# P1's results on a second queue, B21 cast earlier, kept blocks in u's place, four operands not kept (soft mixture of experts)

## The chip, the cores and the metric

One core of a Trainium2 chip runs the whole kernel; seven more cores are idle. The metric is the device time of one execution in microseconds, of which several are taken. Before: a median of 1366.94 us over 3 runs (1365.35 to 1368.19).

The engines have names in the profile: PE (TensorE, matmuls; PEld its weight loads), DVE (VectorE), ACT (ScalarE), POOL (GpSimd), SP (SyncE, which only issues transfers). Transfers are issued from three queues, those of SP, ACT and POOL. Each engine and each queue works in the order of the program.

## The reference

```python
probs = softmax(router_logits)              # 16 x 512 tokens, 8 experts
output = zeros((16, 512, 2048))
for e in range(8):
    output += probs[:, :, e:e+1] * (x @ expert_weights[e])     # 512 -> 2048
```

Since the experts' results are added, this is one matrix product: an operand of 8192 tokens by 8 x 512 columns (x times the token's probability for each expert) with the 4096 x 2048 stacked weights. x, the probabilities and the weights are float32; the kernel multiplies in float16 and adds in float32.

## The kernel before

**Seven products in place of eight.** The product is cut in two in each direction (tokens: even and odd blocks of 256; experts: 0 to 3 and 4 to 7; columns: two halves of 1024), and Winograd's form of Strassen's scheme makes seven products of these quarters, here called P1 to P7 (`r` in the code). `product(r, q)` makes product r for token pair q (0 to 15). Each of these is cut once more into seven: its `steps` 1, 5, 6, 2, 7, 3, 4, each of eight matmuls with 512 columns, write the results (0,0), (0,1), (1,0), (1,1) of 128 tokens by 512 columns. Where two products of a stage allow it, steps 1 and 5 are cut a third time (`Third`): matmuls of 256 columns, with sums `s` of the left operands and `t` of the weights, and between them evacuations of one half of a bank onto the other (`ps<-ps,d` in the profile, parts x6, q6, x7, q7). Part x7 writes into the bank that the evacuation of x6 reads, so it waits for it.

**Stages.** A stage is one or two products, whose steps alternate; each step is a slot, so `(3,4)` is slot 4 of stage 3. `add` numbers the stages: P1 in stages 0 to 7, P2 from 6 to 14, P5 and P6 from 15 (`k5`) to 31 (`k7`), P7 and P4 from 31 to 47 (`k3`), P3 from 47 to 55. Stages 0 to 5, 8 to 13 and 49 to 54 have the third cut; in them the two last slots of the stage before are run between the parts (`held`). P1's operands come from x and the probabilities; P1 for q = 0 and 1 has been made before stage 0.

**Order.** The order on TensorE is written out. Transfers are hung on slots with `at(stage, slot, ...)`. VectorE's work that isn't an evacuation goes through a queue of tasks (`later`) with a planned cost; `slack` runs tasks from it as long as a planned clock of VectorE is behind that of TensorE, so a stage's operands are made during the stage before. Loads of x and probabilities (`start_loads`) are issued two stages ahead.

**What the change touches.**

- `sink` in `product`, r == 1: P1's four results of each product go to DRAM (`kept`), from POOL's queue, as soon as they are evacuated: (0,0) at step 2 and (1,0) at step 4 by ScalarE (`L627`), (1,1) and (0,1) at steps 7 and 3 by VectorE. P2 and P6 read them again.
- `Base.fetch`: reads such a block from SP's queue into an `h` tile (`half()`, 13 places, which hold results on their way out too). P2 and P6 add to it.
- tag `u`, one place of 4 KB in each partition: in P1 a room for loads of x (stages 3 to 5), in P7 and P3 the second product of an operand that is a difference. In P2 and P6 it is free.
- `cast21`, `CASTS`: the weights B21 are cast from float32 to float16 on their way in, from POOL's queue, in eight halves; P2's sums read them in stage 5. `wedge` loads two more halves of weights into one tile of 15 places (`w`), makes t1 and t2 of them on VectorE, and stores these; `WEDGES` says when: the first cast at its first pair of numbers, the second cast so many slots later as its last number says, the two tasks t1 and t2 at the pair between.
- `cast_odd`: casts of single halves, among them B21's block (0,1) again in stage 14.
- `KEEP` and `Left.store`: P6's left operand is a difference that P3 needs too. For q in `KEEP` both its halves (512 KB each) are stored in P6 from SP's queue and fetched again in P3 (`Operand`, 1 MB, from ScalarE's queue into a `w` tile), and P3 makes each half of its operand with two operations (`first`, `less`: product, difference). For other q, `left_of` takes the last line: four blocks are loaded (`xpool`, nine places), and each half takes three operations (`first`, `second` into `u`, `less`).

Of the kernel before, what the change touches and what calls it, by code (L numbers as in the profile page):

```python
# [31 lines left out]
def kernel(  # L32
# [7 lines left out]
    nc = tc.nc  # L40
    P = 128
    f16 = mybir.dt.float16
    f32 = mybir.dt.float32
# [33 lines left out]
    def half():  # L77
        return h_tile([P, NB], f32)
# [21 lines left out]
    def note(i):  # L100
        last[i.ins.engine] = i.ins
        if ordered[0]:
            tc.keep_in_program_order(i)
# [20 lines left out]

    def pool(o, i, **how):
        note(nc.gpsimd.dma_start(out=o, in_=i, **how))  # L126

    def bank():
        return psum.tile([P, NB], f32, name="ps", tag="ps")
# [433 lines left out]
    class Operand:  # L563
# [5 lines left out]
        def fetch(self):  # L569
            self.t = wpool.tile([P, 2, K8, HQ], f16, name="o", tag="w")  # L570
            note(nc.scalar.dma_start(out=self.t, in_=self.source))
# [160 lines left out]
    class Base:  # L732
# [2 lines left out]
        def __init__(self, source):  # L735
            self.source, self.t = source, {}

        def fetch(self, tn):
            self.t[tn] = half()
            sp(self.t[tn], self.source(tn))  # L740

        def __call__(self, tn):
# [16 lines left out]
    right = {r: Right() for r in (2, 5, 6, 7, 4, 3)}  # L759
    right[1] = Right(w, {p: Task(2.2, sums[p]) for p in (6, 7, 4)})  # L760
    lefts, xs, ps_, bases = {}, {}, {}, {}
    KEEP = range(1, 14)

    def xblock(h):
        if h not in xs:
# [34 lines left out]
    def product(r, q, **how):  # L800
        left, loads = left_of(r, q)
        lefts[r, q] = left
        p = None
        if r == 1:
            def sink(tn, o):
                pool(kept_rows(q)(tn), o)
            p = Product(right[1], left, sink)
        elif r == 2:
            if q >= 13:
                base = products[1, q].o.__getitem__  # L810
            else:
                base = bases[2, q] = Base(kept_rows(q))
            p = Product(right[2], left, to_out(q, 0, 0), base)
        elif r == 5:
            bases[6, q] = m1 = Base(kept_rows(q))
            m1.task = {}

            p = Product(right[5], left, to_out(q, 1, 0))
        elif r == 6:
            m1 = bases[6, q]  # L820

            def base(tn):
                need(m1.task[tn])
                return m1.t[tn]
            p = Product(right[6], left, to_out(q, 0, 1), base)
            if q in KEEP:
                left.kept = dram.tile([P, 2, K8, HQ], f16, name=f"kept_left_{q}")
        elif r == 7:
            if q < 14:
                base = bases[7, q] = Base(lambda tn: out_rows(q, 0, 1, tn))  # L830
            else:
                base = products[6, q].o.__getitem__
            p = Product(right[7], left, to_out(q, 1, 1), base)
        elif r == 4:
            p = Product(right[4], left, to_out(q, 1, 0, accum_op=ADD), products[7, q].o.__getitem__)
# [112 lines left out]
        for n in range(end, len(slots)):  # L948
            held.append(lambda n=n: one(n))

    def fetch_at(stage, slot, base, *tns):
        for tn in tns:
            at(stage, slot, lambda tn=tn: base.fetch(tn))


    for q in range(2, 14, 2):
# [3 lines left out]
    forget(*range(0, 26, 2))  # L960
    rest = [15] + list(range(13))
    for i in range(0, 14, 2):
        k = add(product(2, rest[i]), product(2, rest[i + 1]))
        for slot, tn in zip((8, 10, 12, 13), INNER):
            for q in rest[i:i + 2]:
                if q < 13:
                    fetch_at(k if tn == (1, 0) else k - 1, 3 if tn == (1, 0) else slot, bases[2, q], tn)
    xs.clear()
    k5 = add(product(5, 0), product(5, 1))
    add(product(6, 0))  # L970
# [24 lines left out]
    for q in range(16):  # L995
        k = k5 + 1 + q
        duo = len(stages[k - 1]) == 2
        for slot, tn in zip((2, 4, 6, 8) if duo else (1, 2, 3, 4), INNER):
            fetch_at(k - 1, slot, bases[6, q], tn)
        for tn, where in zip(INNER, ((k - 1, 12), (k - 1, 13), (k - 1, 13), (k, 3)) if duo  # L1000
                             else ((k - 1, 5), (k - 1, 6), (k - 1, 6), (k, 3))):
            at(*where, lambda q=q, tn=tn: joined(q, tn))
        if q < 14:
            for slot, tn in zip((7, 9, 11, 17), INNER):
                fetch_at(k7 + q + 1 + slot // 14, slot % 14, bases[7, q], tn)
# [39 lines left out]
    def cast21(kn, e):  # L1045
        if e == 0:
            b21[kn] = new_w()
        cast_w(21, kn, e, b21[kn][:, ds(e * C, C), :])

    for i, kn in enumerate(((0, 0), (0, 1), (1, 1), (1, 0))):  # L1050
        for e in range(2):
            at(*((i + 0,5), (i + 0,12))[e], lambda kn=kn, e=e: cast21(kn, e))

    def sums_at(stage, slot, r, of, ps):
        def go():
# [6 lines left out]
    sums_at(5, 6, 2, b21, (6,))  # L1062
    sums_at(5, 8, 2, b21, (7,))
    sums_at(5, 12, 2, b21, (4,))
    WEDGES = ((3,3,(3,11),4),(4,3,(4,11),4),(5,3,(5,11),4),(6,2,(6,11),4),(7,5,(7,11),1),(8,2,(8,11),4))
    for i, (kn, e) in enumerate((kn, e) for kn in ((0, 0), (1, 0), (1, 1)) for e in range(2)):
        wedge_at(*WEDGES[i][:2], kn, e, *WEDGES[i][2:])

# [48 lines left out]
        return one(4, b[1, 0], b[1, 0], b[1, 1]) if all_ else sixth  # L1117

    last2 = k5 - 1
    for stage, slot, q, e in ((8,9,12,0),(8,13,12,1),(9,4,11,0),(9,9,11,1),(10,2,22,0),(10,7,22,1),(14,8,21,0),(14,12,21,1)):  # L1120
        at(stage, slot, lambda q=q, e=e: cast_odd(q, e))
    at(11,8, odd_t)
    for i, kn in enumerate(((0, 0), (1, 1), (1, 0))):
# [130 lines left out]
    ends = []  # L1254
    HALVES = "2a", "2b"

    def act_dma(o, i):
        note(nc.scalar.dma_start(out=o, in_=i))

    def step_at_end(p, step=finish.step):  # L1260
        if p not in HALVES:
            return step(p)
# [91 lines left out]
```

## Time and profile before

| what | us |
| --- | --- |
| median of 3 runs | 1366.94 |
| lowest, highest run | 1365.35, 1368.19 |
| the profiled execution, its own time | 1364.2 |
| its span, first to last instruction | 1362.4 |
| granted clock of TensorE | 0.999 |

The profile is of one execution. Its page begins with each engine's busy time, goes on with the span in 40 slices, and has the chain that ended last, the costliest groups of instructions and the transfers. Other answers from the same trace are the waits (who waited for whom), windows (busy times in a stretch of the span), and the timeline (instructions in order; x8 at the end of a line means eight of a kind in a row, and in brackets stands how long the engine was idle before and what ended that). A line number is that of a helper: L132 is every matmul, L112 every operation of VectorE with two operands, L126 every transfer from POOL, L123 every plain one from SP. So groups are told apart by their tiles (`kept<-h`). These two slices of the page show how even the load is:

```profile
PE   9999999999999999999999999999999999999998
DVE  7975889989899887888987989888889797998873
```

### The profile page before, as it was taken

How to read it: one execution, taken by the hardware profiler on the slowest of the kernel's cores; microseconds unless marked ns; L12 is line 12 of the kernel's file. 1: busy time of each engine (PE TensorE's matmuls, PEld its weight loads, DVE VectorE, ACT ScalarE, POOL GpSimd, SP SyncE). 2: the span in 40 equal slices, each digit the busy share in tenths (PEclk: the TensorE clock that was granted, in tenths of full speed). 3: DMA queues.
4: the chain of work that ended last, by engine and by line, in shares of the span. 5: the costliest groups of instructions: out<-in, count | busy, mean ns of one | idle time of the engine just before them, and what ended most of it. 6: DMA issues, size and time to landing. Idle time of an engine off the chain costs nothing.

```text
span 1362.4 us, 18627 instructions
## 1 busy us (share of the span) xinstructions
PE 1354.7 (99%) x6825; PEld 664.8 (49%) x6825; DVE 1154.9 (85%) x1432; ACT 204.8 (15%) x390; POOL 415.8 (31%) x650
## 2 busy tenths in 40 slices
PE   9999999999999999999999999999999999999998
PEld 4555545555544444444444444444444444456564
DVE  7975889989899887888987989888889797998873
ACT  3332311111011111111111100000000000123221
POOL 3123333321213342433323222332333322232232
PEclk9999999999999999999999999999999999999999
DMA  9999999998899999999999987988898979989896
GB/s 194 229 259 225 285 229 281 276 302 312 266 310 280 299 320 275 319 309 304 300 302 318 362 307 202 226 242 209 231 241 232 242 212 290 294 224 238 199 211 110
DMA packets 198091, 356.43 MB, mean 262 GB/s; under 512 B 53232, under 2 KB 90352, under 8 KB 193648
## 3 DMA queue, kind: packets, MB, share of 16 engines
q0 software_dynamic: 90448, 183.02, 56.6%
q1 hardware_dynamic: 99488, 132.25, 32.6%
q10 hardware_dynamic: 8064, 39.99, 7.9%
q8 instruction: 53, 0.87, 0.3%
q14 instruction: 38, 0.31, 0.1%
HBM read 217.61 MB, written 167.97 MB: 283 GB/s over the span
## 4 chain that ended last, share of the span: by engine, by line
PE 98%; DMA 1%; DVE 0%; issue 0%; POOL 0%; ACT 0%; DVEq 0%; POOLq 0%
PE ps L132 98%; DMA w<-in_expert_weights_dram 1%; DVE z L112 0%; POOL w L126 0%; DVE ps L112 0%; ACT h L627 0%; POOL kept L126 0%; ACT h L1278 0%; POOL ident L216 0%; DVE w L112 0%; DVEq L112 0%; POOLq L216 0%; POOLq L1338 0%
## 5 line engine op out<-in xcount | busy, mean ns | idle before, releaser
L132 PE MATMUL ps<-w,z 128*128 128x512 f16 x5128 | 1093.6, 373 | 0.1
L132 PEld LDWEIGHTS <-z 128*128 128x128 f16 x5272 | 515.7, 98 | 574.2 <-DMA w<-in_expert_weights_dram 0.3
L126 POOL DMA_DIRECT2D out_dram<-h x380 | 249.4, 663 | 713.9 <-ACT h L638 346.9
L112 DVE TENSOR_TENSOR h<-ps,h 128x512 f32<-128x512 f32 x415 | 283.9, 687 | 139.9 <-PE ps L132 123.5
L112 DVE TENSOR_TENSOR z<-xT,pT 128x2048 f16<-128x2048 f16 x216 | 261.9, 1218 | 5.8 <-DMA kept_left<-z 2.9
L132 PE MATMUL ps<-w,d 128*128 128x512 f16 x880 | 199.1, 379 | 0.0
L132 PEld LDWEIGHTS <-d 128*128 128x128 f16 x880 | 86.1, 98 | 100.1 <-issue 0.2
L112 DVE TENSOR_TENSOR z<-z,d 128x2048 f16<-128x2048 f16 x110 | 131.8, 1217 | 0.0
L112 DVE TENSOR_TENSOR w<-w 128x1024 f16<-128x1024 f16 (+2 forms) x103 | 108.6, 1063 | 13.8 <-DMA w<-in_expert_weights_dram 9.6
L638 ACT COPY h<-ps 128x512 f32<-128x512 f32 x64 | 37.6, 587 | 480.4 <-PE ps L132 465.8
L627 ACT COPY h<-ps 128x512 f32<-128x512 f32 x90 | 52.8, 587 | 284.1 <-PE ps L132 258.8
L112 DVE TENSOR_TENSOR d<-z 128x1024 f16<-128x1024 f16 x110 | 74.3, 687 | 1.6
L126 POOL DMA_DIRECT2D w<-in_expert_weights_dram x77 | 57.2, 754 | 50.5 <-DMA wd<-w 35.8
L624 ACT COPY h<-ps 128x512 f32<-128x512 f32 x90 | 51.7, 590 | 130.1 <-PE ps L132 115.4
L126 POOL DMA_DIRECT2D wd<-w x90 | 53.1, 605 | 46.3 <-DVE w L112 28.7
L132 PEld LDWEIGHTS <-s 128*128 128x128 f16 x576 | 56.3, 98 | 12.9 <-issue 2.8
L126 POOL DMA_DIRECT2D kept<-h x56 | 30.9, 551 | 100.8 <-ACT h L627 70.4
L132 PE MATMUL ps<-t,s 128*128 128x256 f16 x432 | 58.9, 273 | 2.2 <-DVE ps L112 2.2
L112 DVE TENSOR_TENSOR ps<-ps,d 128x256 f32<-128x256 f32 x72 | 30.2, 431 | 24.6 <-PE ps L132 24.5
L112 DVE TENSOR_TENSOR ps<-ps,h 128x512 f32<-128x512 f32 (+1 forms) x66 | 45.2, 688 | 4.7 <-PE ps L132 4.5
L112 DVE TENSOR_TENSOR h<-h 128x512 f32<-128x512 f32 (+2 forms) x69 | 45.1, 675 | 2.5 <-DMA out_dram<-h 2.4
L112 DVE TENSOR_TENSOR u<-xT,pT 128x2048 f16<-128x2048 f16 x38 | 46.3, 1217 | 0.0
(61 smaller groups left out, 354.1 us busy)
## 6 DMA issues: line engine op xcount, KB each, us to landing
out_dram<-h POOLq DMA_DIRECT2D x380, 256.0 KB, 7.0
pT<-p_dram SPq DMA_DIRECT2D x125, 256.0 KB, 6.6
h<-kept SPq DMA_DIRECT2D x116, 256.0 KB, 7.6
w<-wd ACTq DMA_DIRECT2D x25, 1024.0 KB, 9.7
xT<-x SPq DMA_DIRECT2D x76, 256.0 KB, 6.9
wd<-w POOLq DMA_DIRECT2D x76, 256.0 KB, 6.1
w<-in_expert_weights_dram POOLq DMA_DIRECT2D x35, 512.0 KB, 9.7
h<-out_dram SPq DMA_DIRECT2D x60, 256.0 KB, 5.4
```

The source lines that it names most:

```text
L112: dve(nc.vector.tensor_tensor(out=o, in0=a, in1=b, op=op))
L126: note(nc.gpsimd.dma_start(out=o, in_=i, **how))
L132: note(nc.tensor.matmul(ps, z, w, start=start, stop=stop, skip_group_check=True))
L624: act(nc.scalar.copy(o[tn], q if p == 5 else x))
L627: act(nc.scalar.copy(o[TN[p]], b if p == 2 else x))
L638: act(nc.scalar.copy(o[tn], b))
```

## The change

- P1's results (0,0) and (1,0), which ScalarE evacuates, are stored from ScalarE's queue; (0,1) and (1,1) stay on POOL's.
- B21's eight casts stand in stages 0 to 2 in place of 0 to 3. The first wedge's casts stand at slots 1 and 4 of stage 3 in place of 3 and 7. The two casts of B21's block (0,1) in stage 14 stand at slots 3 and 8 in place of 8 and 12.
- Two of the blocks that SP reads back go into `u`'s place in place of two `h` tiles: in P2 block (0,0) of both products of three stages, in P6 blocks (0,0) and (1,1) of the products with odd q up to 13.
- P6's operands for q = 2, 4, 6, 8 are neither stored nor fetched; P3 makes them from x and the probabilities.

```diff
+    def act_dma(o, i):
+        note(nc.scalar.dma_start(out=o, in_=i))
...
-        def fetch(self, tn):
-            self.t[tn] = half()
+        def fetch(self, tn, pair=None):
+            if pair is None:
+                self.t[tn] = half()
+            else:
+                if not pair:
+                    two = zpool.tile([P, 2, NB], f32, name="r", tag="u", bufs=1)
+                    pair += [two[:, i] for i in range(2)]
+                self.t[tn] = pair.pop()
             sp(self.t[tn], self.source(tn))
...
-    KEEP = range(1, 14)
+    KEEP = (1,3,5,7,9,10,11,12,13)
...
             def sink(tn, o):
-                pool(kept_rows(q)(tn), o)
+                (act_dma if tn[1] == 0 else pool)(kept_rows(q)(tn), o)
...
     for i in range(0, 14, 2):
+        pair = [] if i // 2 in (1,3,5) else None
...
-                    fetch_at(k if tn == (1, 0) else k - 1, 3 if tn == (1, 0) else slot, bases[2, q], tn)
+                    fetch_at(k if tn == (1, 0) else k - 1, 3 if tn == (1, 0) else slot, bases[2, q], tn,
+                             pair=pair if tn == (0, 0) else None)
...
+        pair = [] if q in range(1, 14, 2) else None
         for slot, tn in zip((2, 4, 6, 8) if duo else (1, 2, 3, 4), INNER):
-            fetch_at(k - 1, slot, bases[6, q], tn)
+            fetch_at(k - 1, slot, bases[6, q], tn, pair=pair if tn in ((0, 0), (1, 1)) else None)
...
+    CASTS = ((0,5),(0,11),(1,3),(1,8),(1,12),(2,4),(2,9),(2,13))
     for i, kn in enumerate(((0, 0), (0, 1), (1, 1), (1, 0))):
         for e in range(2):
-            at(*((i + 0,5), (i + 0,12))[e], lambda kn=kn, e=e: cast21(kn, e))
+            at(*CASTS[2 * i + e], lambda kn=kn, e=e: cast21(kn, e))
...
-    WEDGES = ((3,3,(3,11),4),(4,3,(4,11),4),(5,3,(5,11),4),(6,2,(6,11),4),(7,5,(7,11),1),(8,2,(8,11),4))
+    WEDGES = ((3,1,(3,11),3),(4,3,(4,11),4),(5,3,(5,11),4),(6,2,(6,11),4),(7,5,(7,11),1),(8,2,(8,11),4))
...
-    for stage, slot, q, e in ((8,9,12,0),(8,13,12,1),(9,4,11,0),(9,9,11,1),(10,2,22,0),(10,7,22,1),(14,8,21,0),(14,12,21,1)):
+    for stage, slot, q, e in ((8,9,12,0),(8,13,12,1),(9,4,11,0),(9,9,11,1),(10,2,22,0),(10,7,22,1),(14,3,21,0),(14,8,21,1)):
```

(The last definition of `act_dma`, further down, goes, since it now stands above.)

More of the change, by code (lines that the diff above doesn't have):

```diff
@@ L949, in run, with fetch_at @@
             held.append(lambda n=n: one(n))
-    def fetch_at(stage, slot, base, *tns):
+    def fetch_at(stage, slot, base, *tns, pair=None):
         for tn in tns:
-            at(stage, slot, lambda tn=tn: base.fetch(tn))
+            at(stage, slot, lambda tn=tn: base.fetch(tn, pair))
     for q in range(2, 14, 2):
@@ L1255 @@
     HALVES = "2a", "2b"
-    def act_dma(o, i):
-        note(nc.scalar.dma_start(out=o, in_=i))
     def step_at_end(p, step=finish.step):
```

## The prediction

> **What bounds the kernel now.** I read the head of the page first, then the waits of TensorE, because only what TensorE waits for can be won back.
>
> ```profile
> span 1362.4 us, 18627 instructions
> PE 1354.7 (99%) x6825; PEld 664.8 (49%) x6825; DVE 1154.9 (85%) x1432; ACT 204.8 (15%) x390; POOL 415.8 (31%) x650
> PE ps L132 <- DVE ps L112: 2.2, 2, 2.0
> PE ps L132 <- DVE h L112: 0.2, 1, 0.2
> ```
>
> TensorE is busy for 99% of the span. Its two waits for a vector operation on a bank (`ps`) make 2.2 us, the longer one 2.0; the one other in this view that lies behind the warm-up is 0.2. The timeline of TensorE shows both, the first around 137, the second around 1209:
>
> ```profile
> 135.60 1.89 PE L132 MATMUL ps<-w,z 128*128 128x512 f16 x8
> 139.53 1.03 PE L132 MATMUL ps<-t,s 128*128 128x256 f16 x8 [2.04 <-DVE ps L112]
> 1206.53 1.04 PE L132 MATMUL ps<-t,s 128*128 128x256 f16 x8
> 1207.40 1.89 PE L132 MATMUL ps<-w,z 128*128 128x512 f16 x8
> 1209.46 1.03 PE L132 MATMUL ps<-t,s 128*128 128x256 f16 x8 [0.17 <-DVE ps L112]
> ```
>
> Undisturbed groups overlap by 0.17 (1206.53 + 1.04 = 1207.57, the next starts at 1207.40), so the two stalls are worth 2.04 + 0.17 = 2.21 and 0.17 + 0.17 = 0.34. Everything else runs at TensorE's pace. P6, the part with most transfers, has no idle time on TensorE at all (a window, its length, then each engine's busy time):
>
> ```profile
> core 0: us, PE busy (x) PEld busy (x) DVE busy (x) ACT busy (x) POOL busy (x), PEclk, DMA share, GB/s
> 443.00:616.00 173.00, 173.00 (x803) 78.47 (x802) 144.54 (x183) 25.77 (x45) 61.67 (x107) 1.00 1.08 306
> ```
>
> So the most that this change can win in the profiled execution is 2.21 + 0.34 = 2.55 us, and it can lose much more. A difference under 0.2% (2.7 us) can't be told from none by a measurement of this kernel.
>
> **The first stall, and what the stores do to it.** The chain of waits gives its cause. From the store of a P1 result on GpSimd's queue it goes to a weight cast, which takes 13.30 to land, and from there to the vector operation on the cast tile:
>
> ```profile
> 122.83 0.43 POOL kept L126
> 123.38 13.30 DMA w<-in_expert_weights_dram
> ```
>
> On VectorE that operation (t2 of the first wedge) and one tile `i` stand ahead of the evacuation that TensorE needs:
>
> ```profile
> 136.78 1.23 DVE L112 TENSOR_TENSOR w<-w 128x2048 f16<-128x2048 f16 x1 [5.44 <-DMA w<-in_expert_weights_dram]
> 137.92 1.22 DVE L112 TENSOR_TENSOR z<-z,d 128x2048 f16<-128x2048 f16 x1
> 139.05 0.76 DVE L112 TENSOR_TENSOR ps<-ps,d 128x256 f32<-128x256 f32 x2
> ```
>
> GpSimd's queue in that stage (stage 3, about 107 to 130) shows why the cast went out only at 123.38:
>
> ```profile
> 108.88 1.46 POOL L126 DMA_DIRECT2D u<-in_x_dram  x2
> 110.33 0.77 POOL L126 DMA_DIRECT2D w<-in_expert_weights_dram  x1
> 111.55 0.56 POOL L126 DMA_DIRECT2D kept<-h  x1 [0.46 <-ACT h L627]
> 115.03 0.56 POOL L126 DMA_DIRECT2D kept<-h  x1 [2.91 <-ACT h L627]
> 115.58 1.53 POOL L126 DMA_DIRECT2D w<-in_expert_weights_dram  x2
> 122.83 0.57 POOL L126 DMA_DIRECT2D kept<-h  x1 [5.71 <-ACT h L627]
> 123.38 0.75 POOL L126 DMA_DIRECT2D w<-in_expert_weights_dram  x1
> ```
>
> All three stores in these rows that wait for ScalarE (L627: results (0,0) and (1,0)) are of the kind that moves. With the wedge's casts at slots 1 and 4 and the last B21 cast at (2,13), nothing that waits for an evacuation is left ahead of them: two x loads, wedge cast, B21 cast, wedge cast. The last goes out at 108.88 + 1.46 + 2 x 0.77 = 111.9 instead of 123.38. Even with the same 13.30 to land it is there at 125.2. The stall is gone if it lands before 136.7 - 2.2 = 134.5; that leaves 9 us for a wait on a free `w` place or a slower queue. I take -2.2; the bounds are -2.2 and 0 (the cast held up otherwise). What is late next is the second wedge, whose operation waits too, but not TensorE behind it; its cast also stands behind moved stores:
>
> ```profile
> 158.47 1.23 DVE L112 TENSOR_TENSOR w<-w 128x2048 f16<-128x2048 f16 x1 [1.50 <-DMA w<-in_expert_weights_dram]
> ```
>
> The Trainium skill (DMA: Bandwidth & Descriptors, section "Issuing engines are not separate DMA queues") speaks against the move: whichever engine issues them, transfers run on the same 16 DMA engines, and a second issuing engine saves only issue time. By that alone the cast would land no earlier and the sum would be short by these 2.2 us. The 5.71 us of idle time in the row are time in which the cast was not issued at all, so I hold the rule true of the transfers and not of this wait.
>
> **ScalarE's side.** 14 products store two blocks there, 28 of the 56, which also takes 28 x 0.55 = 15.4 us off GpSimd:
>
> ```profile
> L126 POOL DMA_DIRECT2D kept<-h x56 | 30.9, 551 | 100.8 <-ACT h L627 70.4 <-DVE h L112 26.7 <-issue 2.8
> 1358.67 0.37 ACT L1278 COPY h<-ps 128x256 f32<-128x256 f32 x1 [2.30 <-PE ps L132]
> 1359.07 0.34 ACTq L1258 DMA_DIRECT2D out_dram<-h  x1
> 102.20:136.20 34.00, 8.83 (x19) 1.00 1.14 225
> ```
>
> An issue right behind its copy, as at the kernel's end, costs ScalarE 0.34 and no wait for another engine: 28 x 0.34 = 9.5 us of issues, beside which ScalarE is busy for 8.83 of 34.00 in a P1 window. Its 19 operations there take 0.46 each on average; a step of eight matmuls lasts 1.89 - 0.17 = 1.7 (rows at 135.60 and 1207.40), and one copy and one store, 0.8, fit in it. I take 0. Without that cover it is 9.5 us at most; a gain beyond the stall isn't there, since nothing else in P1 makes TensorE wait. Queued behind a store that waits on ScalarE would be the next copies, and behind them TensorE's banks.
>
> **The casts.** The same eight casts run up to a stage earlier and hold their tiles longer. No operand is needed before stage 5. GpSimd may now wait for a free tile in place of an evacuation, and loads beside the earlier casts may be slower: the second wedge above had 1.50 us of such a wait with no stall, the first 5.44 with one of 2.21. I take 0, with 0 to 2 us. The cast of B21's other block goes from (14,8) to (14,3), where VectorE is full (33.86 of 34.00), but is not read before stage 15: 0, or the same 2 us if its loads crowd others there.
>
> ```profile
> 374.70:408.70 34.00, 33.86 (x32) 1.00 1.00 310
> ```
>
> **P3 without four kept operands.** For q = 2, 4, 6, 8 the operand's two halves take three vector operations each instead of two: product, second product into `u`, difference.
>
> ```profile
> L112 DVE TENSOR_TENSOR u<-xT,pT 128x2048 f16<-128x2048 f16 x38 | 46.3, 1217 | 0.0
> 1181.20:1205.40 24.20, 23.96 (x30) 1.00 1.00 251
> 1205.40:1229.70 24.30, 22.91 (x29) 1.00 0.85 225
> 1229.70:1253.10 23.40, 19.70 (x24) 1.00 0.94 224
> 1253.10:1276.50 23.40, 19.70 (x24) 1.00 0.92 226
> 1276.50:1299.90 23.40, 19.70 (x24) 1.00 0.93 227
> 1208.98 0.76 DVE L112 TENSOR_TENSOR ps<-ps,d 128x256 f32<-128x256 f32 x2
> 1215.09 0.69 DVE L112 TENSOR_TENSOR s<-z 128x1024 f16<-128x1024 f16 x1
> 1226.37 0.60 PE L132 MATMUL ps<-t,s 128*128 128x256 f16 x4
> ```
>
> That is 2 x 1.22 = 2.44 us in each of the first four windows, 9.7 in all. Length less busy time leaves them idle for 0.24, 1.39, 3.70 and 3.70. Behind by 2.2 after the first, 3.2 after the second, 2.0 after the third, 0.7 after the fourth, VectorE is level again in the fifth. That backlog is work made ahead: sums `s` started at 1215.09 are read at 1226.37, 11 us later, so 3.2 us late is no stall of itself. What costs is a stage that begins with VectorE behind, as now at 1208.98: the evacuation could have begun at 1207.6, came 1.4 late, and cost 0.34, so about 1.05 us are free. Two more stages would now begin so: 2 x 0.34, I take +0.6. The lower bound is 0. The upper is that none of the idle time can be filled, since it stands just ahead of evacuations: 2.44 in the first stage, 2.44 - 1.05 in the next three, 6.6.
>
> The loads for these products are four 256 KB blocks instead of two and a 1 MB operand, and go through nine places. They go out when a product's second half has been made, some 10 us before use by the order of the makes:
>
> ```profile
> pT<-p_dram SPq DMA_DIRECT2D x125, 256.0 KB, 6.6
> ```
>
> At a median of 6.6 to land that is 3 us of room: 0. Without it VectorE waits in order and the 6.6 above come nearer.
>
> **P6 and `u`.** Eight 512 KB stores on SP's queue go (and later four 1 MB fetches on ScalarE's); seven pairs in P6 and three in P2 read into `u`. TensorE waits for nothing in P6 (443 to 616 above), so there is nothing to win: 0. A pair has to wait until the one before, two stages earlier, has been stored; SP waits there in order, with the loads of later stages behind it, as it does today for other places. Those are used over ten slots (17 us) later. I take 0; 2 us if stores are late.
>
> ```profile
> SPq L123 <- DMA out_dram<-h: 204.4, 58, 19.5
> ```
>
> **Sum.** -2.2 + 0.6 = -1.6 against the profiled execution's own 1364.2 (its span 1362.4 and 1.8 around it): 1362.6. The median of the runs, 1366.94, lies 2.7 above that execution, and I keep this distance: 1365.3.
>
> **Rivals.**
> - The stall in ordinary runs is longer than in the profiled one. It hangs on the landing of one cast (13.30) on a busy queue; if the 2.7 us between profile and median stand there, they go too: 1366.9 - 2.7 - 2.2 + 0.6 = 1362.6, faster. For it: nothing else in the trace can vary so easily. Against: start and end can vary too.
> - P3 pays in full (+6.6): 1366.9 - 2.2 + 6.6 = 1371.3, slower by 0.3%. Place: the start of stages 49 to 52 (from 1202 on), at the evacuation after x6. It decides once VectorE is over 1.05 us behind there. For it: 23.96 of 24.20 in the first window. Against: 3.70 of idle time from the third on.
> - The stores move and the cast comes no earlier, since the queue's transfers or a missing tile hold it: 1366.9 + 0.6 = 1367.5, no difference. The rule above, from the Trainium skill, would give this.
>
> **How the numbers follow.** The forecast has 0.47, the longer stall 0.25, P3 in full 0.18, no earlier cast 0.10. Faster by over 0.2% is the first rival and a part of the forecast's scatter: 0.30. Slower is P3 in full and some of the last two with the 2 us of the casts or of `u` on top: 0.24. Between lies 0.46. The forecast's own range is 1363.5 to 1367.5 (bounds of the first stall, scatter of the runs); for 8 in 10 it reaches to the first rival and most of the way to P3 in full: 1362.2 to 1369.6.
>
> **What would show it.** Right: no wait of TensorE near 137; the last wedge cast of stage 3 issued before 113; half of `kept<-h` on ScalarE's queue with no longer gaps between its copies; VectorE without idle time from 1181 to about 1250, and waits of TensorE of some 0.3 at 1230 or 1253. Wrong: waits of TensorE over 1 us at the start of stages 49 to 52; VectorE waiting for `xT` or `pT` there; a new wait between 372 and 443 or in P6.

## The result, and the profile after

The changed kernel takes 1378.94 us (median of 4 runs, 1377.44 to 1382.19) against 1367.19 for the kernel before (4 runs, 1365.35 to 1368.19): a ratio of 1.0091 with a 95% interval of 1.0069 to 1.0112. It is slower by 0.9%; the prediction said 1365.3, with 8 chances in 10 for 1362.2 to 1369.6. The profiled execution took 1382.19, the longest of the four.

The head of its page and the waits of TensorE (us in total, times, longest), then the waits of ScalarE:

```profile
span 1380.4 us, 18591 instructions
PE 1358.2 (98%) x6825; PEld 665.8 (48%) x6825; DVE 1163.7 (84%) x1440; ACT 204.5 (15%) x390; POOL 399.9 (29%) x622
```

```profile
PE ps L135 <- ACT ps L623: 9.8, 1, 9.8
PE ps L135 <- DVE ps L112: 5.3, 3, 2.3
PE ps L135 <- DVE h L112: 2.2, 3, 1.3
...
```

```profile
ACT ps L623 <- DMA pT<-p_dram: 11.2, 1, 11.2
```

ScalarE, which was to issue its stores at no cost, stands for 11.2 us once, and TensorE behind it for 9.8. What ScalarE waited for is strange: its copy of a bank (L623) has nothing to do with `pT`, an operand that SP loads. The chain of waits and ScalarE's timeline give the place, in stage 1:

```profile
65.81 12.82 DMA pT<-p_dram
...
78.71 0.33 ACTq L129
...
79.13 0.58 ACT ps L623
...
79.75 316.07 PE ps L135 x1728
```

```profile
67.34 0.58 ACT L630 COPY h<-ps 128x512 f32<-128x512 f32 x1 [2.89 <-PE ps L135]
78.71 0.33 ACTq L129 DMA_DIRECT2D kept<-h  x1
79.13 1.06 ACT L623 COPY ps<-ps 128x512 f32<-128x512 f32 x2 [11.20 <-DMA pT<-p_dram]
```

The result (1,0) is copied at 67.34 and done by 67.92. Its store ought to go out there. It goes out at 78.71, right after `pT`, issued at 65.81, has landed (65.81 + 12.82 = 78.63). So it isn't the copy behind the store that waits for `pT` but the store: in the trace's semaphore events the transfers of SP and ScalarE take turns on eight completion semaphores (GpSimd's have eight of their own), and the issue of a transfer waits until the one before it on its semaphore has landed. ScalarE works in order; the two copies of banks behind the store come 11.2 us late, and TensorE's timeline shows the price:

```profile
68.89 1.04 PE L135 MATMUL ps<-t,z 128*128 128x256 f16 x8
79.75 6.28 PE L135 MATMUL ps<-w,d 128*128 128x512 f16 x16 [9.82 <-ACT ps L623]
85.87 10.31 PE L135 MATMUL ps<-w,z 128*128 128x512 f16 x47
```

After the pause the 16 matmuls take 6.28 instead of 3.62 (the 47 behind them take 10.31, 0.216 from start to start), so the wait costs 2.7 us more than its length.

To compare kernels I add up, from TensorE's timeline, how far each start of a matmul comes after the one before beyond the undisturbed distance (0.214 for 512 columns, 0.107 for 256; differences over 0.04 counted, so matmuls at a lower rate are included; the first 20 us, with some 3 us of starting up in every kernel, are left out). Span minus this sum is 1359.2 here and 1359.5 before (in all kernels below 1359.2 to 1360.4): whatever the change does shows as such stalls. They are 21.2 in place of 2.9:

| where | before | after |
| --- | --- | --- |
| stage 1, ScalarE | 0 | 12.6 |
| 137, first wedge | 2.2 | 0 |
| 433, stage 15 | 0.1 | 1.9 |
| 585 to 612, P6 | 0 | 4.1 |
| about 1187 | 0.1 | 1.1 |
| P3 | 0.4 | 1.4 |

(At 1187 VectorE waits for a result's store to free an `h` tile; mended has this too, after_again has not. Which part of the change it belongs to stays open.)

The stall at 137 is gone. GpSimd's queue issues the last three casts of stage 3 together, and VectorE's t1 and t2 (`w<-w`), which started at 129.52 and 136.78 before and stand later here by the stall in stage 1, no longer wait for a load:

```profile
122.94 2.26 POOL L126 DMA_DIRECT2D w<-in_expert_weights_dram  x3
```

```profile
142.13 1.22 DVE L112 TENSOR_TENSOR w<-w 128x2048 f16<-128x2048 f16 x1
...
143.86 1.22 DVE L112 TENSOR_TENSOR w<-w 128x2048 f16<-128x2048 f16 x1
```

P6 is one of the places that I had costed at nothing. SP's own queue, VectorE and TensorE:

```profile
560.55 1.03 SPq L123 DMA_DIRECT2D pT<-p_dram  x2
579.60 0.80 SPq L123 DMA_DIRECT2D r<-kept  x2
...
588.70 0.90 SPq L123 DMA_DIRECT2D h<-kept  x1
```

```profile
594.44 0.69 DVE L112 TENSOR_TENSOR h<-h 128x512 f32<-128x512 f32 x1 [2.39 <-DMA h<-kept]
...
602.65 0.69 DVE L112 TENSOR_TENSOR h<-h 128x512 f32<-128x512 f32 x1 [1.05 <-DMA h<-kept]
```

```profile
598.67 3.61 PE L135 MATMUL ps<-w,d 128*128 128x512 f16 x16 [2.31 <-DVE ps L112]
...
606.99 5.34 PE L135 MATMUL ps<-w,z 128*128 128x512 f16 x24 [1.26 <-DVE h L112]
```

SP does nothing from 561.6 to 579.6. It waits for `u`'s place, which the pair before holds until it is stored, as the waits of SP's queue say (us in total, times, longest):

```profile
SPq L123 <- DMA out_dram<-r: 45.2, 5, 17.9
```

The kept blocks behind it come late, VectorE waits for them, and TensorE for VectorE. P3 follows under the points of the prediction.

### The profile page after: what moved, and what is told of

It is laid out like the page before. It is cut to its first block, busy times and chain, and to the rows that moved or that the text cites. A ratio compares the mean times of both kernels' runs of the same rounds, so it can differ in the third digit from the quotient of the medians.

```text
span 1380.4 us, 18591 instructions
## 1 busy us (share of the span) xinstructions
PE 1358.2 (98%) x6825; PEld 665.8 (48%) x6825; DVE 1163.7 (84%) x1440; ACT 204.5 (15%) x390; POOL 399.9 (29%) x622
## 4 chain that ended last, share of the span: by engine, by line
PE 87%; DMA 5%; issue 4%; DVE 3%; POOL 1%; SPq 0%; ACT 0%; ACTq 0%; POOLq 0%; DVEq 0%
PE ps L135 87%; DVE z L112 1%; DMA pT<-p_dram 1%; DMA h<-kept 1%; DMA out_dram<-h 1%; POOL out_dram L126 1%; DVE h L112 1%; DMA xs<-in_x_dram 1%; DMA wd<-w 1%; PE every L94 0%; DMA xT<-x 0%; DVE d L112 0%; SPq L466 0%; DVE w L112 0%; DVE ps L112 0%
## 5 line engine op out<-in xcount | busy, mean ns | idle before, releaser
L126 POOL DMA_DIRECT2D out_dram<-h x360 | 238.1, 665 | 632.0 <-ACT h L641 249.1
L112 DVE TENSOR_TENSOR h<-ps,h 128x512 f32<-128x512 f32 x401 | 274.0, 687 | 128.3 <-PE ps L135 107.1
L630 ACT COPY h<-ps 128x512 f32<-128x512 f32 x90 | 52.7, 586 | 292.7 <-PE ps L135 284.5
L641 ACT COPY h<-ps 128x512 f32<-128x512 f32 x51 | 29.9, 586 | 435.1 <-PE ps L135 434.0
L627 ACT COPY h<-ps 128x512 f32<-128x512 f32 x90 | 51.7, 590 | 131.5 <-PE ps L135 118.4
L112 DVE TENSOR_TENSOR u<-xT,pT 128x2048 f16<-128x2048 f16 x46 | 56.0, 1217 | 0.0
L112 DVE TENSOR_TENSOR z<-z,u 128x2048 f16<-128x2048 f16 x42 | 51.1, 1218 | 0.3
L126 POOL DMA_DIRECT2D kept<-h x28 | 15.5, 554 | 116.7 <-DVE h L112 116.6
L112 DVE TENSOR_TENSOR h<-h 128x512 f32<-128x512 f32 (+3 forms) x55 | 36.2, 674 | 10.6 <-DMA h<-kept 9.8
```

Source lines behind the costliest of these rows:

```text
L112: dve(nc.vector.tensor_tensor(out=o, in0=a, in1=b, op=op))
L627: act(nc.scalar.copy(o[tn], q if p == 5 else x))
L630: act(nc.scalar.copy(o[TN[p]], b if p == 2 else x))
L641: act(nc.scalar.copy(o[tn], b))
```

## The experiments

Two theories stood at the start. **A**: ScalarE's stores are what costs, since ScalarE waits in order at them with evacuations behind it. **B**: it is the transfers, which come at other times or more of them together (casts, pairs, P3's loads). Every kernel ran beside the kernel before; those of one table part share its runs. The columns give the stalls of the profiled execution, added up as above, by place: in P1 ahead of 130 (ScalarE's place), at the wedges (130 to 200), near 300 to 320, in stage 15 (410 to 440), in P6 (540 to 640) and in P3 (1200 to 1250).

| kernel | median (range) | ratio, 95% interval | P1 | wedges | 300 | st. 15 | P6 | P3 |
| --- | --- | --- | --- | --- | --- | --- | --- | --- |
| before, first profile | 1366.94 | | 0 | 2.3 | 0 | 0.1 | 0 | 0.4 |
| changed | 1378.94 (1377.4 to 1382.2) | 1.0091, 1.0069 to 1.0112 | 12.6 | 0 | 0 | 1.9 | 4.1 | 1.4 |
| *beside before at 1367.23* | | | | | | | | |
| only_stores | 1376.78 (1373.6 to 1378.6) | 1.0061, 1.0042 to 1.0079 | 9.9 | 4.2 | 1.7 | 0.1 | 0.3 | 0.4 |
| only_casts | 1372.97 (1370.8 to 1377.8) | 1.0042, 1.0026 to 1.0058 | 0 | 3.0 | 1.8 | 4.0 | 0 | 0.4 |
| only_pairs | 1364.99 (1363.2 to 1370.9) | 0.9977, 0.9961 to 0.9994 | 0 | 2.1 | 0 | 0.1 | 5.3 | 0 |
| only_keep | 1368.37 (1365.3 to 1373.6) | 1.0010, 0.9993 to 1.0026 | 0 | 0.4 | 2.0 | 0.1 | 0 | 1.4 |
| *beside before at 1366.81* | | | | | | | | |
| stores_late | 1374.38 (1366.1 to 1380.7) | 1.0048, 1.0021 to 1.0075 | 0 | 5.2 | 0 | 5.2 | 0 | 1.4 |
| no_stores | 1373.44 (1367.1 to 1377.2) | 1.0045, 1.0028 to 1.0062 | 0 | 6.4 | 0 | 3.6 | 0 | 1.4 |
| only_14 | 1369.64 (1366.3 to 1376.8) | 1.0023, 1.0001 to 1.0045 | 0 | 4.6 | 1.7 | 4.8 | 0 | 0.1 |
| mended | 1378.75 (1375.4 to 1381.4) | 1.0079, 1.0053 to 1.0104 | 8.1 | 5.5 | 0 | 0.1 | 5.0 | 0.4 |
| *beside before at 1365.74* | | | | | | | | |
| sp_stores | 1370.79 (1368.4 to 1373.5) | 1.0035, 1.0012 to 1.0057 | 0 | 8.5 | 1.5 | 0.1 | 0.4 | 0 |
| pairs_p2 | 1367.34 (1364.0 to 1369.7) | 1.0010, 0.9994 to 1.0025 | 0 | 1.8 | 0 | 0.1 | 0 | 0.2 |
| pairs_p6 | 1370.12 (1368.4 to 1373.2) | 1.0039, 1.0019 to 1.0058 | 0 | 7.4 | 1.4 | 1.5 | 0 | 0.4 |
| pairs_casts | 1368.45 (1363.8 to 1372.6) | 1.0019, 1.0006 to 1.0032 | 0.4 | 4.8 | 0 | 0.1 | 5.7 | 0.1 |
| *beside before at 1366.93* | | | | | | | | |
| after_again | 1378.83 (1375.2 to 1382.5) | 1.0077, 1.0053 to 1.0100 | 10.3 | 0.3 | 0 | 2.8 | 0 | 1.2 |
| after_sp | 1370.37 (1364.7 to 1377.5) | 1.0021, 1.0001 to 1.0042 | 0 | 7.1 | 0 | 0.9 | 0 | 1.4 |
| pairs_again | 1368.34 (1362.6 to 1370.6) | 0.9995, 0.9979 to 1.0011 | 0 | 2.1 | 0 | 0.1 | 4.8 | 0 |
| before_again | 1367.27 (1365.0 to 1375.8) | 1.0005, 0.9987 to 1.0022 | 0 | 3.0 | 1.2 | 0.1 | 0 | 0.2 |

**Each part alone.** Four kernels: the kernel before with the stores, the casts, the pairs or the kept operands of the change, and nothing else.

```diff
-                pool(kept_rows(q)(tn), o)
+                (act_dma if tn[1] == 0 else pool)(kept_rows(q)(tn), o)
```

> The kernel before with P1's results (0,0) and (1,0) stored from ScalarE's queue, nothing else. Theory A (the store itself waits: on ScalarE it can't be issued until an earlier transfer of SP, the pT that landed at 78.63, has landed, and the copies behind it wait too): TensorE stalls by 5 to 10 us in stage 1 near 70, with slow matmuls behind it, 1372 to 1379. Theory B (the earlier casts crowd the loads, and it is these that make the pT land 12.8 us after its issue): no such stall, the one at 137 gone, 1364 to 1367.

```diff
-            at(*((i + 0,5), (i + 0,12))[e], lambda kn=kn, e=e: cast21(kn, e))
+            at(*CASTS[2 * i + e], lambda kn=kn, e=e: cast21(kn, e))
...
-    WEDGES = ((3,3,(3,11),4),(4,3,(4,11),4),(5,3,(5,11),4),(6,2,(6,11),4),(7,5,(7,11),1),(8,2,(8,11),4))
+    WEDGES = ((3,1,(3,11),3),(4,3,(4,11),4),(5,3,(5,11),4),(6,2,(6,11),4),(7,5,(7,11),1),(8,2,(8,11),4))
...
-    for stage, slot, q, e in ((8,9,12,0),(8,13,12,1),(9,4,11,0),(9,9,11,1),(10,2,22,0),(10,7,22,1),(14,8,21,0),(14,12,21,1)):
+    for stage, slot, q, e in ((8,9,12,0),(8,13,12,1),(9,4,11,0),(9,9,11,1),(10,2,22,0),(10,7,22,1),(14,3,21,0),(14,8,21,1)):
```

> The kernel before with the casts of B21, the first wedge and the block in stage 14 moved, nothing else; P1's results stay on GpSimd's queue. Theory A: no stall in stage 1, 1364 to 1368; the stall at 137 goes, since two of the three casts of stage 3 come earlier. Theory B: the loads of stage 1 are late as in the changed kernel, VectorE waits for them over 5 us and TensorE over 2 us, 1370 or more.

```diff
-            fetch_at(k - 1, slot, bases[6, q], tn)
+            fetch_at(k - 1, slot, bases[6, q], tn, pair=pair if tn in ((0, 0), (1, 1)) else None)
```

(and the same in P2)

> The kernel before with two blocks read into u's place, nothing else. Theory C (SP waits in order until the pair before has been stored, 18 us from 561 on in the changed kernel, and the loads behind it are late): waits of TensorE of 3 to 6 us in sum between 420 and 620, 1370 to 1373. Rival (those stalls came from the changed times of P1 or from fewer kept operands): under 1 us there, 1366 to 1368.

```diff
-    KEEP = range(1, 14)
+    KEEP = (1,3,5,7,9,10,11,12,13)
```

> The kernel before with P6's operands 2, 4, 6, 8 not kept, nothing else. Theory D (VectorE is late by 1 to 1.4 us at the start of stage 49 alone): the wait near 1209 grows from 0.17 to 1.0 to 1.5, 1367.5 to 1369. Rival (P3 pays at four stages): 3 to 6 us of waits from 1205 to 1280, 1370 to 1373.

The stores alone cost 9.5 us (1376.78 - 1367.23), the casts 5.7, the kept operands 1.1; the pairs gained 2.2. The sum, 14.2, is near the whole (11.8), so the parts mostly add up. Theory A has the largest part but not all. The casts and the pairs fit neither of their expectations: the casts leave 2.4 us of stall at 137 and lose most in stage 15 (4.0), and the profiled execution of the pairs stalls for 5.3 in P6 though their median is the lowest of all. That execution took 1369.42; eight of the ten lie between 1363.2 and 1365.6. The stores alone show the same stop at the same place as the whole change, TensorE's timeline:

```profile
77.74 5.86 PE L135 MATMUL ps<-w,d 128*128 128x512 f16 x16 [7.50 <-ACT ps L623]
```

**Where the stores hurt, and the rest of the change without them.** If only stage 1 were at fault, leaving its stores with GpSimd should do; a second kernel leaves all stores there.

```diff
-                (act_dma if tn[1] == 0 else pool)(kept_rows(q)(tn), o)
+                (act_dma if tn[1] == 0 and q >= 6 else pool)(kept_rows(q)(tn), o)
```

> The changed kernel, but the results of q below 6 (stages 0 and 1) go from GpSimd's queue again; those of q from 6 on stay on ScalarE's. Theory A (a store on ScalarE waits for the landing of an earlier SP transfer, and that only hurts where loads land late, in stage 1): no wait of TensorE for ScalarE, 11 to 13 us less than the changed kernel, 1366 to 1368. Rival (any store on ScalarE hurts, it is found a place later): a new wait of TensorE for ScalarE over 3 us in stages 2 to 7, 1371 or more.

```diff
-                (act_dma if tn[1] == 0 else pool)(kept_rows(q)(tn), o)
+                pool(kept_rows(q)(tn), o)
```

> The changed kernel with all of P1's results stored from GpSimd's queue. Theory A: no wait for ScalarE near 70; what is left are the cast of stage 14 (about 4 us near 420) and 0 to 4 us from u in P6, 1368 to 1373. Rival (the parts only hurt together): 1365 to 1367.

Both shed the stop of ScalarE in their profiles and both still lie 0.5% above before, by stalls at the wedges, in stage 15 and in P3 (so the 1366 to 1368 expected of the first was missed). A third kernel takes the late stores once more and mends what the other parts had shown: stage 14's casts where they were, all operands kept.

```diff
-    KEEP = (1,3,5,7,9,10,11,12,13)
+    KEEP = range(1, 14)
...
-                (act_dma if tn[1] == 0 else pool)(kept_rows(q)(tn), o)
+                (act_dma if tn[1] == 0 and q >= 6 else pool)(kept_rows(q)(tn), o)
...
-    for stage, slot, q, e in ((8,9,12,0),(8,13,12,1),(9,4,11,0),(9,9,11,1),(10,2,22,0),(10,7,22,1),(14,3,21,0),(14,8,21,1)):
+    for stage, slot, q, e in ((8,9,12,0),(8,13,12,1),(9,4,11,0),(9,9,11,1),(10,2,22,0),(10,7,22,1),(14,8,21,0),(14,12,21,1)):
```

> The changed kernel, with the results of q below 6 from GpSimd's queue, the casts of stage 14 back at slots 8 and 12, and all operands from 1 to 13 kept. Theories A and E: no stall near 70, none near 137, none near 420, the one near 1209 back at 0.2; 1362 to 1365, faster than the kernel before. Rival (the blocks in u's place cost P6 4 us in most executions): 1366 or more.

It failed as a mend (1378.75) and settled the place. ScalarE's and TensorE's timelines in stage 2:

```profile
101.30 0.59 ACT L630 COPY h<-ps 128x512 f32<-128x512 f32 x1 [1.14 <-PE ps L135]
115.27 0.36 ACTq L129 DMA_DIRECT2D kept<-h  x1
115.67 0.36 ACT L715 COPY ps<-ps 128x256 f32<-128x256 f32 x1 [13.78 <-DMA xT<-u]
```

```profile
116.08 1.86 PE L135 MATMUL ps<-w,z 128*128 128x256 f16 x8 [4.43 <-ACT ps L715]
```

The store of a result copied at 101.30 goes out at 115.27; this time it waited for a transpose on SP's queue (`xT<-u`). So it isn't stage 1: any store on ScalarE's queue can meet a late load of SP's. stores_late has the same stores in these stages and in its profile no such wait, so whether one is met varies from run to run; its runs scatter over 14.6 us.

**In order on ScalarE, or the transfers?** The decisive pair keeps every transfer and moves only who issues the 28 stores: SP, on whose queue no evacuation waits. First on the kernel before, then on the changed one, beside the changed one itself and the kernel before itself.

```diff
-                pool(kept_rows(q)(tn), o)
+                (sp if tn[1] == 0 else pool)(kept_rows(q)(tn), o)
```

> The kernel before, with P1's results (0,0) and (1,0) stored from SP's queue in place of ScalarE's; nothing else is changed. Theory A (what costs is that ScalarE, which evacuates banks, waits in order at a store for an earlier transfer): the waits are on SP now, no wait of TensorE for ScalarE (L623) appears in stages 0 to 4, and the time lies within 0.3% of before (1363 to 1371); if SP's loads come late behind the waits, TensorE waits for VectorE instead, 2 to 4 us. Theory B (the stores hurt as such, by the place or time at which their transfers run): 1374 to 1379 as with the stores on ScalarE alone, 0.5 to 0.8% slower.

```diff
-                (act_dma if tn[1] == 0 else pool)(kept_rows(q)(tn), o)
+                (sp if tn[1] == 0 else pool)(kept_rows(q)(tn), o)
```

> The changed kernel with the 28 stores issued from SP's queue in place of ScalarE's, every transfer the same. Theory A (ScalarE waits in order at a store, and TensorE's banks behind it): no wait of TensorE for ScalarE in P1, and 1369 to 1373, 6 us or more below the changed kernel, near the change with all stores left on GpSimd's queue (1.0045). Theory B (the stores' transfers hurt by themselves): within 3 us of the changed kernel.

> The changed kernel as it is, once more, beside the next one. Both theories: 1.008 to 1.010 of before (1378), with a wait of TensorE for ScalarE (L623 or L715) of 4 us or more somewhere in stages 1 to 4.

> The kernel before without any edit, compared with itself. If executions differ only at random: 1.000, with an interval that holds 1. If a load of a program sets part of the time (the stall near 137 was 2.2 us in one profile and 5.5 in another whose instructions are the same up to there): up to 0.3% either way, and the small ratios of the other experiments say nothing below that.

The changed kernel takes 1378.83 again, and 1370.37 with SP as issuer: 8.5 us less with the same transfers. In the profile of the latter ScalarE goes on at once after the copy at 67.38, and the store stands in SP's queue:

```profile
67.38 0.59 ACT L630 COPY h<-ps 128x512 f32<-128x512 f32 x1 [2.89 <-PE ps L135]
68.69 0.57 ACT L623 COPY ps<-ps 128x512 f32<-128x512 f32 x1 [0.72 <-DVE ps L112]
```

```profile
66.13 2.18 SPq L123 DMA_DIRECT2D kept<-h  x2
```

That is theory A, shown for this part. On the kernel before the same exchange saves less: 1370.79 (1.0035) with SP, a little over the 0.3% expected, against 1376.78 (1.0061) with ScalarE. No wait for ScalarE is left there, but 8.5 us at the wedges; about half the loss of the stores goes with the issuer and half stays.

What stays fits theory B. In the changed kernel with no stop in stage 1 TensorE stops at the second wedge, for casts that GpSimd issued only at 151.51. GpSimd in the kernel before, then GpSimd, VectorE and TensorE of the changed kernel with SP's stores:

```profile
147.29 0.76 POOL L126 DMA_DIRECT2D w<-in_expert_weights_dram  x1 [6.83 <-DMA wd<-w]
...
148.99 0.77 POOL L126 DMA_DIRECT2D w<-in_expert_weights_dram  x1
```

```profile
151.51 1.53 POOL L126 DMA_DIRECT2D w<-in_expert_weights_dram  x2 [16.02 <-issue]
```

```profile
160.10 1.23 DVE L112 TENSOR_TENSOR w<-w 128x2048 f16<-128x2048 f16 x1 [7.00 <-DMA w<-in_expert_weights_dram]
```

```profile
165.85 1.87 PE L135 MATMUL ps<-t,s 128*128 128x256 f16 x8 [4.99 <-DVE ps L112]
```

GpSimd itself was late: its chain of waits goes back through the store of the first wedge's t1, and the semaphore events name the store of t2 after it. The times to landing of these two stores (`wd<-w`, issued between 128 and 152), in the kernel before and then here:

```profile
DMA to landing us min/median/max: 8.7/9.5/10.4
```

```profile
DMA to landing us min/median/max: 13.3/14.2/15.1
```

The tile of the first wedge has to be stored before a cast can take its place. In the kernel before the store of t2 goes out at 138.30 and has landed at 147.01; here it goes out at 134.75 and lands at 149.81. In the four other kernels that lose the stall at 137 without a stop in P1 it is the same: issued at 133.5 to 136.4, landed at 147.9 to 150.4. So an earlier t2 doesn't free the tile any earlier. What slows these stores is not shown; sp_stores, whose casts are not moved, has it too.

**Stage 14 by itself.**

```diff
-    for stage, slot, q, e in ((8,9,12,0),(8,13,12,1),(9,4,11,0),(9,9,11,1),(10,2,22,0),(10,7,22,1),(14,8,21,0),(14,12,21,1)):
+    for stage, slot, q, e in ((8,9,12,0),(8,13,12,1),(9,4,11,0),(9,9,11,1),(10,2,22,0),(10,7,22,1),(14,3,21,0),(14,8,21,1)):
```

> The kernel before with the two casts of stage 14 at slots 3 and 8, nothing else. Theory E (the cast goes out ahead of three 1 MB fetches and takes a weight tile that the second was to have; these land up to 12 us later, VectorE waits 3.8 us for one and has no idle time to make it up): TensorE waits 3 to 5 us between 415 and 430, 1370 to 1372, all that moving the casts costs. Rival (the casts of stages 0 to 2 cost it): under 1 us there, 1366 to 1368.

1.0023, and 4.8 us of stall in stage 15. In the kernel before, the cast goes out behind three fetches of 1 MB; the timelines of GpSimd and of ScalarE's queue:

```profile
386.90 0.77 POOL L126 DMA_DIRECT2D w<-in_expert_weights_dram  x1
```

```profile
378.31 3.36 ACTq L180 DMA_DIRECT2D w<-wd  x3
```

In only_14 it goes ahead of them (all else stands 4.8 us later here, by the stalls further ahead); the timelines of GpSimd, ScalarE's queue, VectorE and TensorE:

```profile
380.22 0.76 POOL L126 DMA_DIRECT2D w<-in_expert_weights_dram  x1 [1.11 <-PE ps L132]
```

```profile
383.63 3.60 ACTq L180 DMA_DIRECT2D w<-wd  x3
```

```profile
405.57 2.29 DVE L112 TENSOR_TENSOR w<-w 128x4096 f16<-128x4096 f16 x1 [3.06 <-DMA w<-wd]
```

```profile
431.38 3.47 PE L132 MATMUL ps<-w,d 128*128 128x512 f16 x8 [2.40 <-DVE ps L112]
```

The three fetches land 8.6 to 17.4 us after their issue in the kernel before, 15.2 to 26.0 us after it here. VectorE, full in this stretch, loses 3.06 to a fetch and makes it up only after TensorE has stood. In the seven profiles with this move stage 15 stalls for 0.9 to 5.2 us; in the eleven without it for 0.1, once for 1.5.

**The pairs, and whether something beats the kernel before.** The gain of the pairs alone was tried by its halves (P2, P6), with the earlier casts (without stage 14's), and once more as it was.

```diff
-                    fetch_at(k if tn == (1, 0) else k - 1, 3 if tn == (1, 0) else slot, bases[2, q], tn)
+                    fetch_at(k if tn == (1, 0) else k - 1, 3 if tn == (1, 0) else slot, bases[2, q], tn,
+                             pair=pair if tn == (0, 0) else None)
```

> The kernel before with only the kept blocks of P2 read into u's place (three pairs). If the gain of the pairs alone (0.9977) comes from P2: 0.997 to 0.999, and no wait of TensorE in P6 (443 to 616) in any case. If it comes from P6: 1.000.

```diff
-            fetch_at(k - 1, slot, bases[6, q], tn)
+            fetch_at(k - 1, slot, bases[6, q], tn, pair=pair if tn in ((0, 0), (1, 1)) else None)
```

> The kernel before with only the kept blocks of P6 read into u's place (seven pairs). If the gain of the pairs comes from P6, or from the first wedge's stall at 137 (0.86 in place of 2.21 in the profile of the pairs alone, and the pairs do nothing before stage 9): 0.997 to 0.999, with single executions 4 us longer, when SP's wait for the place makes VectorE wait for a kept block near 580 to 605. If the pairs of P6 only cost: 1.000 to 1.003.

```diff
+    CASTS = ((0,5),(0,11),(1,3),(1,8),(1,12),(2,4),(2,9),(2,13))
...
-    WEDGES = ((3,3,(3,11),4),(4,3,(4,11),4),(5,3,(5,11),4),(6,2,(6,11),4),(7,5,(7,11),1),(8,2,(8,11),4))
+    WEDGES = ((3,1,(3,11),3),(4,3,(4,11),4),(5,3,(5,11),4),(6,2,(6,11),4),(7,5,(7,11),1),(8,2,(8,11),4))
```

> The kernel before with the pairs, B21's casts in stages 0 to 2 and the first wedge's casts earlier; the stores stay on GpSimd's queue, stage 14 and the kept operands as before. With the waits of GpSimd behind the evacuations left in place the casts alone left 2.4 us of stall at 137 and added 0.5 at 163, so: 0.998 to 1.000 (1364 to 1367), no better than the pairs alone (1365.0). If the earlier casts do remove the stall: 0.996, 1362. If they crowd P1's loads as in the kernel of all three casts (4 us there from stage 14, 2 us at 305): 1.001 to 1.003.

> The pairs alone, once more on this chip. If they gain: 0.996 to 0.9995 as before. If that was the chip or the load and the halves tell it right: 1.000 to 1.004.

The gain didn't come back (0.9995, interval 0.9979 to 1.0011), nor is it in either half. Five of the ten profiles with P6's pairs lose 4.1 to 5.7 us in P6, the other five nothing; of the eight without them none loses over 0.5. So by the medians the pairs bring nothing, and those of P6 sometimes cost.

The profiles show one thing for the pairs of P2 that the medians don't (column 300). In seven of the eight profiles without them VectorE waits 1.7 to 2.5 us for a `pT` between 300 and 320, and TensorE loses 1.2 to 2.0; in none of the ten with them. These loads of `pT` go out at 295.99 and 297.19 in before_again and at 285.69 and 286.71 in pairs_p2: SP's fetches into `h` just ahead of them take it 16.1 us in the one and 4.2 in the other. The first profile before happened to be without that stall, and a gain of 0.1% is less than the medians can tell (pairs_p2: 1.0010, 0.9994 to 1.0025).

No kernel here beats the kernel before beyond doubt. The kernel before compared with itself gives 1.0005, with an interval of ± 0.2%; smaller differences mean nothing here.

That pairs_p6 lies at 1.0039 is not explained by P6. Its instructions up to stage 15 are those of the kernel before, the cast goes out at 123.34 as it did there (123.38), and yet (VectorE, TensorE):

```profile
139.99 1.22 DVE L112 TENSOR_TENSOR w<-w 128x2048 f16<-128x2048 f16 x1 [8.69 <-DMA w<-in_expert_weights_dram]
```

```profile
142.75 1.87 PE L132 MATMUL ps<-t,s 128*128 128x256 f16 x8 [5.29 <-DVE ps L112]
```

The same instructions wait 8.69 for the cast in place of 5.44. All five of its runs are at 1368.4 or more, so something holds for all of them; what it is stays open.

## Why the prediction was wrong, point by point

**The step that failed: ScalarE's side.** "An issue right behind its copy, as at the kernel's end, costs ScalarE 0.34 and no wait for another engine", taken as 0, with 9.5 us "at most". The row was taken from the end of the kernel, where SP has issued its last load by 1326.6 and the transfer ahead of the store on its semaphore landed at 1312.7, 46 us before; in P1 a store waits for the landing of an earlier transfer of SP's queue, with the next copies behind it. The prediction named what stands behind such a store ("the next copies, and behind them TensorE's banks") but had the store wait for ScalarE alone, and priced 28 issues at 0.34 where one wait of 11.20 decides. Measured: 12.6 us in the first profile after, 10.3 in the second, 8.5 between the medians with the two issuers.

**The stall at 137: right in the changed kernel, and no gain in itself.** -2.2 was taken and came. But the sentence on what is late next, that the second wedge's operation waits and not TensorE behind it, is wrong: in every kernel that removes the first stall without stopping TensorE earlier in P1, TensorE stands at the second wedge (no_stores, stores_late, pairs_casts, sp_stores, after_sp: 3.1 to 5.5 us in one stall near 160). The sentence blamed the moved stores ahead of that cast; what the cast waits for is the landing of the first wedge's t2, before and after. In the changed kernel itself the second wedge costs nothing, in both profiles. That the ten microseconds lost in stage 1 gave its loads the time is a guess: only_stores and mended stop in P1 too and lose 4.2 and 5.5 at the wedges all the same. The issue time itself was right: the last of the three casts starts at 124.4, less the 12.6 of stall 111.8, where 111.9 was predicted.

**The casts.** 0, with up to 2 us, for those in stages 0 to 2; the wedges show no gain (3.0 in only_casts, 2.3 and 3.0 before). Stage 14's move had "0, or the same 2 us if its loads crowd others there". The mechanism was the named one, its size was too small: 0.9 to 5.2.

**P6 and `u`.** "I take 0; 2 us if stores are late": named, and the stores are late in half of the profiles, for 4.1 to 5.7. The ten slots of room were measured from the issue; SP stood for 18 us, longer than these 17. That P2's pairs take away a wait was not foreseen: the one profile before doesn't have it.

**P3.** The place was right and the size near, the working wrong in one step. VectorE has next to no idle time through the first two windows (0.2 and 0.4 us; columns: stretch, length, then busy time of PE, PEld, DVE, ACT and POOL, each with its count, PEclk, DMA share, GB/s), and one stage begins late, at its first evacuation:

```profile
1199.00:1223.20 24.20, 24.20 (x123) 11.86 (x122) 23.99 (x30) 6.55 (x14) 6.92 (x8) 1.00 0.87 187
1223.20:1247.50 24.30, 23.12 (x135) 12.96 (x134) 23.91 (x30) 6.87 (x14) 8.62 (x10) 1.00 0.94 193
1247.50:1271.00 23.50, 23.50 (x138) 13.38 (x137) 20.38 (x25) 6.95 (x14) 6.87 (x8) 1.00 0.88 200
```

```profile
1227.74 1.03 PE L135 MATMUL ps<-t,s 128*128 128x256 f16 x8 [1.18 <-DVE ps L112]
```

0.6 in two more stages was predicted, 1.0 in one came (1.4 in place of 0.4); the wait of 1.18 is over the 1 us that I had named as a sign of being wrong there. P3 in full (6.6) is ruled out. But VectorE does not work off its backlog in the idle time of these windows, as my sum had it. Over the first five it is busy for 107.3 in place of 106.0 us, 1.3 of the 9.8 that were added, and it is idle for 3.1 to 3.9 in each of the last three. What is added pushes work made ahead further back, in the order written out for VectorE, and most of it turns up near the end, the same stretch before and after:

```profile
1323.30:1340.00 16.70, 16.70 (x98) 9.36 (x96) 8.08 (x11) 5.48 (x10) 4.33 (x5) 1.00 0.73 127
```

```profile
1341.20:1357.90 16.70, 16.70 (x99) 9.52 (x98) 13.36 (x15) 5.65 (x10) 4.15 (x5) 1.00 0.75 131
```

**The rivals.** None of the four cases held the result: all put the loss or gain at the wedge or in P3, and the 0.24 for slower stood on P3 in full, the casts and `u`. The first was right in that the stall varies with the same instructions, from 0.4 to 7.4 us at the wedges in the profiles whose P1 is the kernel before's; taking it away didn't bring the gain. The third, that the casts come no earlier in effect, is nearest to what the casts and stores do with an issuer that can wait.

**The Trainium skill's rule** (DMA: Bandwidth & Descriptors, section "Issuing engines are not separate DMA queues"), that transfers of whichever engine share the same 16 DMA engines and a second issuer saves issue time only, was set aside for this wait. It comes out better than I held: taking the stores from GpSimd's queue is slower with either issuer (1.0035 from SP, 1.0061 from ScalarE), and where casts and t2 do come earlier the store of t2 still doesn't land before 147. What the two issuers differ by, 8.5 us in the changed kernel, goes with the stop of ScalarE, not with the transfers.

## What to carry to other kernels

A transfer issued from an engine that also evacuates banks is not priced by its 0.33 us of issue: its issue can wait for an unrelated earlier transfer (11.20 and 13.78 here), and everything behind it on that engine waits too. Price it by the landing times of the other transfers under way, and give it to an engine with nothing urgent behind. When the first of several late loads is moved, work out the next ones as TensorE's stalls, and ask of each move ahead which transfers it goes ahead of (stage 14's cast before three fetches).

## What the runs showed of the hardware that I had not expected

A wait of TensorE can cost more than its length: behind it TensorE may run at half rate for a while. In the first profile after, some twelve matmuls of 512 columns start 0.43 apart in place of 0.216 behind the pause of 9.82, until 85.2, and the granted clock (the third number from the end of a window's line) is 0.50:

```profile
80.00:85.00 5.00, 5.00 (x13) 1.82 (x12) 2.18 (x3) 1.77 (x4) 0.00 (x0) 0.50 1.25 211
```

In the second, after_again, the rate is back 3.8 us behind the pause (timeline of TensorE):

```profile
78.44 5.50 PE L135 MATMUL ps<-w,d 128*128 128x512 f16 x16 [8.26 <-ACT ps L623]
```

Behind the 5.29 us of pairs_p6 eight matmuls of 256 columns take 1.87 in place of 1.03. Over all eighteen profiles, behind the start-up, the half rate follows each of the eleven pauses from 2.9 us on and none under 2.1 us. Between, it goes both ways: behind 2.31 us (the row at 598.67) sixteen matmuls take the usual 3.61, yet behind the 2.40 of only_14 (431.38) eight take 3.47 in place of 1.89, while three other pauses of 2.40 and one of 2.76 (before_again) leave the rate as it was. The shortest pause with half rate behind it is 2.19 (only_pairs). The stretch lasts 2.7 to 5.7 us, so a wait from about 2.2 us on may cost some 1.4 to 2.9 us on top.

The Trainium skill (TensorE: Matmul & The Clock Gate, section "Part 1: The HAM clock gate (the "warmup" mystery)") has this as a rule: the clock is halved after an idle window of about 3.4 us, comes back after as long a busy one, and the windows run freely. The trace agrees on the half rate and on the order of its length (2.7 to 5.7 us); that 2.19 us of idle time sufficed once and 2.40 twice is less than the page's window, and there the measurement decides.

Two transfers with nothing in common but a semaphore delay each other: SP's and ScalarE's share eight in these traces, and a store that was ready at 67.92 went out at 78.71.
